# Nearest-neighbour upsampling on one core: the order of the first two loads

## The chip, the cores and the metric

The kernel runs on one core of a Trainium2 chip. The metric is the device time of one execution in microseconds (us). Beside the timed runs there is one profiled execution, whose records give the rows quoted below.

## The reference

The input is 16 images of 64 channels of 64 x 64 float32 values, 16.8 MB. Every value is repeated twice along both axes, so the output is 16 x 64 x 128 x 128, 67.1 MB. There is no arithmetic, only copying:

```python
new_h, new_w = (h * scale_factor, w * scale_factor)
for i in range(new_h):
    for j in range(new_w):
        result[:, :, i, j] = x[:, :, i // scale_factor, j // scale_factor]
```

## The kernel before

Batch, channel and height are flattened to 65,536 image rows of 64 values (256 bytes). Each of the 128 partitions holds R = 512 consecutive rows, 128 KB, and each input row becomes two output rows of 128 values, 1 KB in all. One tile, mem, holds everything in a partition: a free area of 79 expanded rows at the front and the whole input (xt) behind it.

**Loads (L148 to L151).** SyncE issues three loads, one behind the other on its one DMA queue: rows 0 to 8 of each partition (2 KB per partition, 256 KB in all; HEAD is 8), rows 8 to 256 (63,488 bytes per partition, 7,936 KB) and rows 256 to 512 (65,536 bytes per partition). None waits for anything. Each load is split over the 16 DMA engines, eight partitions to an engine.

**Chunks (L160 to L172).** The rows are worked off in nine chunks of 62, 32, 48, 64, 50, 64, 64, 64 and 64 rows. For each chunk VectorE copies the rows into an expanded block u (L170), reading each value and each row twice by a broadcast, and SyncE issues one store of the block (L171). The first chunk is copied in two parts, rows 0 to 31 and 31 to 62; both must be done before its store. The blocks lie in turn at the front of mem and right below the rows that are still unexpanded, over rows already used, so a copy has to wait until the store that last read its place has landed.

**Order.** The framework derives all semaphores from the data: the first copy (rows 0 to 31) waits for the load of rows 0 to 8 and for that of rows 8 to 256; the second copy (rows 31 to 62) needs the latter alone. All nine stores share SyncE's queue with the loads and follow them there.

**Before and after the body.** begin_before_barrier takes the first three instructions of SyncE (EARLY = 3), the three loads, in their order, and puts them ahead of the barrier at the kernel's start. close_early rewrites the end: all semaphores but that of the last store are waited for and cleared by GpSimd, and SyncE alone waits for the last store.

Of the kernel before, what the change touches and what calls it, by code (L numbers as in the profile page):

```python
# [1 line left out]

# [4 lines left out]

EARLY = 3  # L10


def begin_before_barrier(nc):

    blocks = nc.main_func.blocks
    main, body = blocks[0], blocks[1]
    sp = mybir.EngineType.SP
    loads = [i for i in body.instructions if i.engine == sp][:EARLY]  # L20
    for load in loads:
        assert isinstance(load, mybir.InstDMACopy), type(load)
        assert not (load.sync_info and load.sync_info.on_wait)
    names = [i.name for i in loads]
    body.instructions = [i for i in body.instructions if i.name not in names]
    kept = list(main.instructions)
    at = next(
        n
        for n, i in enumerate(kept)
        if i.engine == sp and isinstance(i, mybir.InstDrain)  # L30
    )
    kept[at:at] = loads
    main.instructions = kept


def close_early(nc):

    blocks = nc.main_func.blocks  # L40
    sp, pool = mybir.EngineType.SP, mybir.EngineType.Pool
    stores = [
        i
        for i in blocks[1].instructions
        if i.engine == sp and isinstance(i, mybir.InstDMACopy)
    ]
    last = stores[-1].sync_info.on_update[0].id

    end = list(blocks[-1].instructions)
    wait = end[0]  # L50
    assert wait.engine == sp and isinstance(wait, mybir.InstDrain)
    waits = list(wait.sync_info.on_wait)
    assert len({w.id for w in waits}) == len(waits) > 2
    assert all(w.wait_mode == "sem-ge-imm" for w in waits)

    mine = [i for i in end if i.engine == pool]
    kinds = [type(i).__name__ for i in mine]
    assert kinds == [
        "InstDrain",
        "InstEventSemaphore",  # L60
        "InstEventSemaphore",
        "InstDrain",
        "InstISA",
        "InstDrain",
        "InstEventSemaphore",
        "InstEventSemaphore",
    ], kinds
    d0, gather0, release0, d1, clear, d2, gather1, release1 = mine


    lo, hi = clear.ant_dict["range_first"], clear.ant_dict["range_last"]
    assert lo <= last <= hi and all(lo <= w.id <= hi for w in waits)
    clears = []
    for a, b in ((lo, last), (last + 1, hi + 1)):
        if a < b:
            clears.append(nc.gpsimd.sem_clear(range(a, b)).ins)

    landed = mybir.InstDrain(
        name=wait.name,
        engine=pool,  # L80
        debug=wait.debug,
        sync_info=mybir.SyncInfo(
            on_wait=[w for w in waits if w.id != last], on_update=[]
        ),
    )
    (w,) = [w for w in waits if w.id == last]
    final = mybir.InstEventSemaphore(
        name=clear.name,
        engine=sp,
        debug=wait.debug,  # L90
        sync_info=mybir.SyncInfo(
            on_wait=[w],
            on_update=[
                mybir.SyncUpdate(
                    sync_type=w.sync_type,
                    id=w.id,
                    ant_name=w.ant_name,
                    update_mode="sem-sub-imm",
                    update_value=w.wait_value,
                )  # L100
            ],
        ),
    )
    others = [i for i in end if i.engine != pool and i is not wait]
    blocks[-1].instructions = others + [
        d0, gather0, release0, gather1, release1, d1, landed, *clears, d2, final
    ]


@with_exitstack  # L110
def kernel(
    ctx: ExitStack,
    tc: tile.TileContext,
    x: bass.AP,
    scale_factor: int,
    out: bass.AP,
):
    nc = tc.nc
    nc.at_finalize(begin_before_barrier)
    nc.at_finalize(close_early)  # L120
    P = nc.NUM_PARTITIONS
    s = int(scale_factor)
    B, C, H, W = x.shape
    R = B * C * H // P
    fdt = x.dtype

    xp = x.rearrange("b c h w -> (b c h) w").rearrange("(p r) w -> p r w", p=P)
    op = out.rearrange("b c (h hd) w -> (b c h) (hd w)", hd=s).rearrange(  # L130
        "(p r) w -> p r w", p=P
    )

    rows = [62, 32, 48, 64, 50, 64, 64, 64, 64]
    GROW = s * s
    FREE = 79
    WF = FREE * GROW * W  # L140
    assert sum(rows) == R
    mem_pool = ctx.enter_context(tc.tile_pool(name="mem", bufs=1))
    mem = mem_pool.tile([P, WF + R * W], fdt, name="mem")
    xt = mem[:, WF:].rearrange("p (r w) -> p r w", r=R)

    HEAD = 8  # L148
    cuts = [0, HEAD, R // 2, R]
    for lo, hi in zip(cuts, cuts[1:]):  # L150
        nc.sync.dma_start(out=xt[:, lo:hi], in_=xp[:, lo:hi])  # L151

    def expanded(r0, r1):
        return (
            xt[:, r0:r1].unsqueeze(2).unsqueeze(4).to_broadcast([P, r1 - r0, s, W, s])
        )

    r0 = 0
    before = (0, 0)
    for n, k in enumerate(rows):  # L160
        size = k * GROW * W
        at = 0 if n % 2 == 0 else WF + r0 * W - size
        assert at >= before[1] or at + size <= before[0]
        before = (at, at + size)
        u = mem[:, at : at + size].rearrange(
            "p (k a w b) -> p k a w b", k=k, a=s, w=W
        )
        parts = [0, 31, k] if n == 0 else [0, k]
        for a, b in zip(parts, parts[1:]):
            nc.vector.tensor_copy(out=u[:, a:b], in_=expanded(r0 + a, r0 + b))  # L170
        nc.sync.dma_start(out=op[:, r0 : r0 + k, :], in_=u)  # L171
        r0 += k  # L172


# [1 line left out]
_INS = ['x', 'scale_factor']  # L176
_OUTS = [((16, 64, 128, 128), 'float32')]

_NUMBERS = {'scale_factor': 2}


# [26 lines left out]
```

## Time and profile before

| What | Value |
|---|---|
| Timed runs | 197.21, 197.22, 197.28 us; median 197.22 |
| Profiled execution | span 195.8 us, first to last instruction; no time of its own around the span is recorded |
| Median less span | 1.4 us |
| HBM | 16.78 MB read, 67.11 MB written |
| VectorE | 78.0 us busy in 10 copies |

Only one profiled execution exists, so its terms are set against its span, and the 1.4 us are taken as a constant between span and timed run. Rows of the chain of waits are: start, duration, what. A row of the DMA view with the words "share of 16 engines" sums the durations of all packets that start in the window and divides by the window's length times 16; a packet belongs to the window in which it starts, so that a short window can show over 100%. A large packet is one partition's part of a transfer. The packets under 512 bytes are the 4-byte completion writes, one for each engine and transfer. The column "us to landing" counts from the issue on SyncE to the last completion.

### The profile page before, as it was taken

The numbers are of one execution on the slowest core, as the hardware profiler recorded it, in microseconds if no ns is written. First come the engines' busy times: TensorE is split into PE (matmuls) and PEld (weight loads), VectorE is DVE, ScalarE is ACT, GpSimd is POOL, SyncE is SP. The second block draws the span as 40 slices with busy tenths as digits, with TensorE's granted clock in tenths as the row PEclk, the third lists the DMA queues.
The fourth block names the chain that finished last, engine by engine and source line by source line (L and its number), as shares of the span: only waits on it lengthen the run. The fifth ranks groups of instructions, "written<-read, shape, count | busy, mean of one in ns | idle before, by whom it ended". The sixth has DMA issues, their size and how long they took to land.

```text
span 195.8 us, 76 instructions
## 1 busy us (share of the span) xinstructions
DVE 78.0 (40%) x10; POOL 0.2 (0%) x4
## 2 busy tenths in 40 slices
DVE  0000599980007579085008907900890088000000
POOL 0000000000000000000000000000000000000000
DMA  9999999999999999899987989999999999999994
GB/s 456 415 428 415 428 428 428 428 415 415 415 415 428 428 482 482 375 469 495 469 384 345 502 348 455 442 469 482 469 442 428 428 428 442 428 428 428 428 428 214
DMA packets 1728, 83.89 MB, mean 428 GB/s; under 512 B 192, under 2 KB 192, under 8 KB 320
## 3 DMA queue, kind: packets, MB, share of 16 engines
q1 hardware_dynamic: 1728, 83.89, 99.2%
HBM read 16.78 MB, written 67.11 MB: 428 GB/s over the span
## 4 chain that ended last, share of the span: by engine, by line
DMA 60%; DVE 24%; SPq 0%; issue 0%; DVEq 0%
DMA out_dram<-mem 49%; DVE mem L170 24%; DMA mem<-in_x_dram 11%; SPq L151 0%; DVEq L170 0%
## 5 line engine op out<-in xcount | busy, mean ns | idle before, releaser
L170 DVE COPY mem<-mem 128x16384 f32<-128x16384 f32 (+4 forms) x10 | 78.0, 7812 | 87.8 <-DMA out_dram<-mem 65.8
L189 POOL MEMSET const-uint8-127<- 128x1 uint8 x1 | 0.1, 102 | 0.0
L189 POOL MEMSET const-bfloat16-1.0<- 128x1 bf16 x1 | 0.1, 101 | 0.0
L189 POOL MEMSET const-float32-0.0<- 128x1 f32 x1 | 0.1, 98 | 0.2 <-issue 0.2
L189 POOL MEMSET const-float32-1.0<- 128x1 f32 x1 | 0.1, 98 | 0.0
## 6 DMA issues: line engine op xcount, KB each, us to landing
mem<-in_x_dram SPq DMA_DIRECT2D x1, 7936.0 KB, 21.5
out_dram<-mem SPq DMA_DIRECT2D x1, 7936.0 KB, 21.2
out_dram<-mem SPq DMA_DIRECT2D x1, 6400.0 KB, 27.6
out_dram<-mem SPq DMA_DIRECT2D x1, 6144.0 KB, 17.5
out_dram<-mem SPq DMA_DIRECT2D x1, 4096.0 KB, 26.4
mem<-in_x_dram SPq DMA_DIRECT2D x1, 256.0 KB, 2.7
out_dram<-mem SPq DMA_DIRECT2D x5, 29.8
mem<-in_x_dram SPq DMA_DIRECT2D x1, 40.4
```

Source lines behind the costliest of these rows:

```text
L170: nc.vector.tensor_copy(out=u[:, a:b], in_=expanded(r0 + a, r0 + b))
L189: nc = _bacc.Bacc("TRN2", target_bir_lowering=False, num_devices=1)
```

## The change

The 2 KB per partition of rows 0 to 8 are issued second instead of first. The load of rows 8 to 256 becomes the first of the queue; the load of rows 256 to 512 stays third. Sizes, destinations, copies, stores and waits on data stay as they are.

```diff
     HEAD = 8
-    cuts = [0, HEAD, R // 2, R]
-    for lo, hi in zip(cuts, cuts[1:]):
+    for lo, hi in ((HEAD, R // 2), (0, HEAD), (R // 2, R)):
         nc.sync.dma_start(out=xt[:, lo:hi], in_=xp[:, lo:hi])
```

## The prediction

> **What bounds the kernel now.** I read the page first, then the chain of waits, then the DMA view cut into narrow windows at the start, at the end of the first half's load and at the end of the kernel. The page:
>
> ```profile
> span 195.8 us, 76 instructions
> DVE 78.0 (40%) x10; POOL 0.2 (0%) x4
> DMA  9999999999999999899987989999999999999994
> DMA packets 1728, 83.89 MB, mean 428 GB/s; under 512 B 192, under 2 KB 192, under 8 KB 320
> q1 hardware_dynamic: 1728, 83.89, 99.2%
> ```
>
> VectorE works 40% of the span; the 16 DMA engines work 99.2% of it, on one queue. The stretches say at what rate (columns: stretch, its length, DVE, POOL, clock, DMA share, GB/s):
>
> ```profile
> 22.00:38.00 16.00, 16.00 (x2) 0.00 (x0) 1.00 1.00 434
> 100.00:190.00 90.00, 34.78 (x4) 0.00 (x0) 1.00 1.00 435
> ```
>
> At 434.5 GB/s the 83.89 MB need 83.89/0.4345 = 193.1 us of the 195.8. Only 2.7 us are not full-rate transfer, and the change can win or lose only by what it does to these or by tearing a hole into the stream. The chain that ended last (start, us, what) shows how the front hangs together:
>
> ```profile
> 0.00 0.38 SPq L151
> 0.43 21.46 DMA mem<-in_x_dram
> 21.99 16.76 DVE mem L170 x2
> 38.77 21.19 DMA out_dram<-mem
> ```
>
> The chain names the 7,936 KB load, issued second at 0.43, landed at 21.89. VectorE then makes the first store's data in two copies (16.76), and that store is issued at 38.77. This reads as if the issue at 0.00 delayed the rest by 0.43. The DMA view says otherwise.
>
> **The change part by part.** First the issue. SyncE issues three loads; the rows are the line's own (duration min/median/max, first and last start) and the landing times:
>
> ```profile
> L151 SPq DMA_DIRECT2D mem<-in_x_dram x3: 380/420/432, 0.0 to 0.9; - x3
> mem<-in_x_dram SPq DMA_DIRECT2D x1, 7936.0 KB, 21.5
> mem<-in_x_dram SPq DMA_DIRECT2D x1, 256.0 KB, 2.7
> mem<-in_x_dram SPq DMA_DIRECT2D x1, 40.4
> ```
>
> The windows from 0 to 0.99 us and from 0.99 to 1.25 us of the DMA view (packets that start there; share of 16 engines):
>
> ```profile
> DMA packets 0, 0.00 MB, mean 0 GB/s; under 512 B 0, under 2 KB 0, under 8 KB 0
> ...
> DMA packets 17, 0.03 MB, mean 134 GB/s; under 512 B 0, under 2 KB 0, under 8 KB 17
> q1 hardware_dynamic: 17, 0.03, 129.3%
> ```
>
> No packet starts for 0.99 us, then 17 do within 0.26 us. The second load is issued at 0.43, so by the same delay its packets could run from about 1.4 on; the 256 KB load is still being moved then (below). So that issue lies beside the first load's start-up and transfer, and taking the 7,936 KB load to the front saves none of the 0.43. The 256 KB load, now issued at about 0.4, has some 20 us of cover before its turn on the engines comes. That a transfer with long rows takes longer from issue to first packet is not shown: the issue rows (380 for the first, at most 432 for the others) bound it at 0.05 us. Issue: 0, bounds 0 and +0.05.
>
> Next the transfer of the head itself. Windows 1.65 to 1.9 us (2 KB packets alone) and 5 to 19 us (63,488-byte packets alone):
>
> ```profile
> DMA packets 43, 0.09 MB, mean 352 GB/s; under 512 B 0, under 2 KB 0, under 8 KB 43
> q1 hardware_dynamic: 43, 0.09, 90.7%
> ...
> DMA packets 96, 6.09 MB, mean 435 GB/s; under 512 B 0, under 2 KB 0, under 8 KB 0
> q1 hardware_dynamic: 96, 6.09, 100.4%
> ```
>
> A 2 KB packet takes 0.25 x 16 x 0.907 / 43 = 0.084 us, a large one 14 x 16 x 1.004 / 96 = 2.343 us. Each engine has 8 of each in the first half: 0.68 + 18.74 = 19.4 us in either order. Moving the head moves 0.68 us of work from before the large packets to behind them, and VectorE's first copy (rows 0 to 31) needs both loads before and after the change. The sum of work changes by 0.
>
> What can change is the start-up loss. Windows 0 to 1.9 us and 0 to 3 us:
>
> ```profile
> q1 hardware_dynamic: 97, 0.20, 43.8%
> ...
> DMA packets 160, 1.28 MB, mean 426 GB/s; under 512 B 16, under 2 KB 16, under 8 KB 144
> q1 hardware_dynamic: 160, 1.28, 118.4%
> ```
>
> The 97 packets that start before 1.9 us, all 2 KB, cost 1.9 x 16 x 0.438 = 13.3 engine-us instead of 97 x 0.084 = 8.2: 5.1 too much, 0.32 us for each engine. (The first 17 cost 0.26 x 16 x 1.293 / 17 = 0.316 each.) The 63 that follow until 3 us hold the last 31 small ones, 16 completion writes and each engine's first large one; they cost 3 x 16 x 1.184 - 13.3 = 43.5, less 31 x 0.084 = 2.6, so 40.9/16 = 2.55 for a first large packet against 2.343: 0.21 lost. Together the start now loses 0.53 us per engine, in two steps: a cold first read, and the step from small to large packets.
>
> With the large packets first there is one cold start. It costs at least what one cold packet loses, 0.316 - 0.084 = 0.23, and at most the whole 0.53, if the second step is no step of size but the 16 engines beginning to pull at full rate together. I take the middle, 0.35 to 0.4, so a gain of about 0.15 (bounds 0 and 0.3). That price comes back in part at the new place: the stream now goes from large to 2 KB packets and from these to 65,536-byte ones. The trace of before has no such passage in a running stream. The nearest rows bound each: 0.00 (share 1.00 in 22 to 38 us, large packets throughout) and 0.21 (the small-to-large step at the start). The descriptors of both loads will have been waiting for 20 us, which puts it nearer to the lower end: I take 0.1 for the two together, bounds 0 and 0.42.
>
> Here a page speaks against the change. The Trainium skill, HBM Reference, section Latency, gives 0.2 us for an access on average and 2 us at high load. The head's reads would then move from an idle memory to a busy one, and if one such read were exposed the sum would be about 1.8 us worse. No row here shows such an exposure: the stretches above run at share 1.00 under full load.
>
> Then the laggard. Windows 20.8 to 21.2, 21.5 to 21.6, 194 to 195.1, 195.1 to 195.4 and 195.4 to 195.8 us; "under 512 B" counts the completion writes, one per engine and transfer:
>
> ```profile
> DMA packets 30, 0.98 MB, mean 2458 GB/s; under 512 B 15, under 2 KB 15, under 8 KB 15
> ...
> DMA packets 2, 0.07 MB, mean 655 GB/s; under 512 B 1, under 2 KB 1, under 8 KB 1
> ...
> DMA packets 14, 0.00 MB, mean 0 GB/s; under 512 B 14, under 2 KB 14, under 8 KB 14
> ...
> DMA packets 1, 0.00 MB, mean 0 GB/s; under 512 B 1, under 2 KB 1, under 8 KB 1
> ...
> DMA packets 1, 0.00 MB, mean 0 GB/s; under 512 B 1, under 2 KB 1, under 8 KB 1
> ```
>
> Fifteen engines finish the first half before 21.2 us, one not before 21.5; at the very end again one comes last, after 195.4. An engine that is 0.3 us late in the first load is 0.3 us late 174 us later: every engine carries its own lag to the end, and the latest sets the span. Where it fell behind shows in the window 2.4 to 2.6 us, with one packet, the last engine's first large one:
>
> ```profile
> DMA packets 1, 0.06 MB, mean 317 GB/s; under 512 B 0, under 2 KB 0, under 8 KB 0
> ```
>
> That lag arose in the first 2.6 us, in the stretch that the change rewrites. With 16 cold starts some engine will be last again; I take its lag as unchanged, bounds -0.3 (it is gone) and +0.3 (twice as long).
>
> Last the wait. VectorE's first copy waited for two semaphores before and does so after; behind it on VectorE are all copies, behind these on SyncE all stores. If the first half lands later than its engines finish, store 1 comes later. Its cover, from the windows 38.77 to 40.1 and 40.1 to 40.5 us, in which the third load ends:
>
> ```profile
> DMA packets 0, 0.00 MB, mean 0 GB/s; under 512 B 0, under 2 KB 0, under 8 KB 0
> ...
> DMA packets 28, 0.89 MB, mean 2222 GB/s; under 512 B 14, under 2 KB 14, under 8 KB 14
> ```
>
> Store 1 is issued at 38.77, with 0.99 ready at 39.76; the first engine is free of load 3 no earlier than 40.1. The cover is at least 0.34 us, and it moves along with the first half, since load 3 queues right behind that. Only a landing later than the stream by more than 0.34 would leave the engines idle. The rest of the kernel is the same instructions at the same distances. Cost 0.
>
> Sum: issue 0, work 0, start -0.15, passages +0.1, laggard 0, wait 0 = -0.05 us. Span 195.8 becomes 195.75; the timed runs of before lie 1.4 above the profiled span (median 197.22, 197.21 to 197.28), so 197.17, said as 197.15. All terms at their low ends give -0.3 - 0.3 = -0.6, all at their high ends 0.05 + 0.42 + 0.3 = +0.77.
>
> **The rivals.** (1) Faster: the lag belongs to the 2 KB start. Large first packets leave one cold start and no late step to large packets, and both the 0.21 and the laggard's 0.3 go: -0.5, 196.7. For it: the lag was born before 2.6 us, at just that step. Against: large reads have to start cold too.
>
> (2) Slower: 2 KB packets amid a saturated stream can't hide their reads behind one another. It sits at 20 to 22 us, on every engine, and costs 0.23 for each of the 8 packets that runs at the cold packet's 0.316 instead of 0.084. Two such packets make +0.46, 197.7; all 8 would make +1.9, 199.1. It decides from two packets on, if the start gains nothing. For it: 0.32 us of the present start is lost just so, on small packets. Against: from 1.65 us on they run at 0.084 one behind another, and deeper in the stream their descriptors are long there.
>
> (3) The chain taken at its word: the large load issued 0.43 earlier lands 0.43 earlier and all behind it follows, 196.8. Against: the head's 0.68 us of work is still ahead of the landing and ahead of load 3. The order itself is sure: the code that moves the three loads ahead of the barrier keeps the order of the list.
>
> (4) The head's completion arrives late, the cover of 0.34 is used up and store 1 leaves a hole: 0.4 us of hole wants a landing 0.75 later, 197.6. Against: completions of the 256 KB and of the 7,936 KB load both come from the same queue at each engine's end, and both gate the copy today.
>
> **How the numbers follow.** A measurement of this kernel can tell about 0.2%, 0.39 us: below 196.83 is faster, above 197.61 slower. The forecast, no change that can be told, gets 0.50. Rival 1 gets 0.20 and rival 3 0.05: faster 0.25. Rival 2 gets 0.20 and rival 4 0.05: slower 0.25. The range, 196.6 to 197.9, reaches over rival 1's price and both bounds of the sum on either side (-0.6 and +0.7) and leaves out the far end of rival 2. The forecast's own range is 196.85 to 197.6.
>
> **What would show it.** Right: first packets again about 1.0 us after the first issue; in the window 0 to 3 us 16 large packets and a cost for each of 2.6 to 2.9; the first half's completions within 0.3 us of 20.8 to 21.6, VectorE's first copy at 21.6 to 22.3; share 1.00 from 22 us on. The start is wrong if the completions come before 20.7 (rival 1 or 3); the passages if the 2 KB packets near 21 us take clearly more than 0.084 (rival 2); the wait if packets of store 1 start only after a gap behind load 3 (rival 4). The prediction as a whole is wrong if the last completion write moves by more than 0.4 us.

## The result and the profile after

The changed kernel takes 197.51 us (median of 21 runs, 197.36 to 197.87) where the kernel before takes 197.18 us (21 runs, 196.93 to 197.61). The ratio is 1.0017 with a 95% interval of 1.0010 to 1.0023: 0.33 us slower. That is inside the 0.2% that the prediction called no change, and inside its range, but the sign is not the forecast one (-0.05 us), and the interval excludes zero.

The page of the changed kernel:

```profile
span 196.2 us, 75 instructions
DVE 78.0 (40%) x10; POOL 0.2 (0%) x4
DMA  9999999999999999899998989999999999999994
q1 hardware_dynamic: 1728, 83.89, 99.1%
mem<-in_x_dram SPq DMA_DIRECT2D x1, 7936.0 KB, 21.3
mem<-in_x_dram SPq DMA_DIRECT2D x1, 256.0 KB, 21.5
```

The span is 0.4 us longer with the same bytes and the same 78.0 us of VectorE. There is one instruction less: a separate wait of VectorE has gone. The chain (start, us, what) says which:

```profile
0.00 21.34 DMA mem<-in_x_dram
21.34 0.02 issue
21.36 16.76 DVE mem L169 x2
38.12 0.02 issue
38.14 22.18 DMA out_dram<-mem
```

VectorE starts at 21.36, as soon as the 7,936 KB load has landed at 21.34, and 0.63 us earlier than before (21.99). The 256 KB load lands later, at 0.43 + 21.5 = 21.9. The framework has swapped the first chunk's two copies. Rows 31 to 62, which need the large load alone, are now copied first, and rows 0 to 31, which need the 2 KB load too, second. Both copies take 8.4 us, so their durations don't show the swap. The start does: a copy that runs at 21.36, half a microsecond before the 256 KB load has landed, can't be the one that reads rows 0 to 8. So the order of the first two copies and the first wait did not stay as the section on the change had them. Store 1 is issued at 38.14 instead of 38.77.

An earlier store would seem to do no harm, and yet it lands later: 22.18 us after the issue instead of 21.19, which is at 60.32 instead of 59.96. Of the 0.99 us, 0.63 are only a longer time in the queue; 0.36 are a real delay. A part of it arises ahead of the store on the engines. The window 37.6 to 38.7 us of the DMA view holds each engine's last packet of load 3, 16 in all, in every kernel here but one; first before, then after:

```profile
DMA packets 16, 1.05 MB, mean 953 GB/s; under 512 B 0, under 2 KB 0, under 8 KB 0
q1 hardware_dynamic: 16, 1.05, 220.2%
```

```profile
DMA packets 16, 1.05 MB, mean 953 GB/s; under 512 B 0, under 2 KB 0, under 8 KB 0
q1 hardware_dynamic: 16, 1.05, 230.1%
```

Share times 1.1 us is the mean duration of one packet: 2.422 us before, 2.531 us after. The engines lose 0.11 us on the mean in their last load packet, at a time when store 1 is already queued behind it. The loss is uneven, and the engine that ends last decides. The packet that starts last of the 16 (one packet each, window 38.4 to 38.5 before and 38.5 to 38.6 after) takes 0.1 x 16 x share, 2.42 us before and 2.70 after:

```profile
q1 hardware_dynamic: 1, 0.07, 151.1%
```

```profile
q1 hardware_dynamic: 1, 0.07, 168.7%
```

The start differs as well. The windows 0.99 to 1.25, 1.25 to 1.5, 1.5 to 2.1 and 0 to 3 us of the changed kernel:

```profile
DMA packets 10, 0.63 MB, mean 2442 GB/s; under 512 B 0, under 2 KB 0, under 8 KB 0
...
DMA packets 3, 0.19 MB, mean 762 GB/s; under 512 B 0, under 2 KB 0, under 8 KB 0
...
DMA packets 3, 0.19 MB, mean 317 GB/s; under 512 B 0, under 2 KB 0, under 8 KB 0
...
q1 hardware_dynamic: 16, 1.02, 99.5%
```

Ten engines start their first packet in the first 0.26 us, three by 1.5 us and three after. A first packet takes 3 x 16 x 0.995 / 16 = 2.98 us where a later one takes 2.34: 0.64 lost, and late starts on top, against 0.53 in all before. The window 21.25 to 21.9 us shows the outcome, before and after ("under 512 B" are completions):

```profile
DMA packets 2, 0.07 MB, mean 101 GB/s; under 512 B 1, under 2 KB 1, under 8 KB 1
```

```profile
DMA packets 30, 0.68 MB, mean 1043 GB/s; under 512 B 9, under 2 KB 9, under 8 KB 20
```

Nine engines end the first half after 21.25, before the change one did. So two causes offer themselves: a start that is worse for most engines, and a store that is queued too early. A third comes from the prediction: the passages into and out of the 2 KB packets, which now stand in the middle of the stream.

### The profile page after: what moved, and what is told of

Read it like the earlier page. It is cut to its first block, busy times and chain, and to the rows that moved or that the text cites. A ratio compares the mean times of both kernels' runs of the same rounds, so it can differ in the third digit from the quotient of the medians.

```text
span 196.2 us, 75 instructions
## 1 busy us (share of the span) xinstructions
DVE 78.0 (40%) x10; POOL 0.2 (0%) x4
## 4 chain that ended last, share of the span: by engine, by line
DMA 60%; DVE 24%; issue 0%
DMA out_dram<-mem 50%; DVE mem L169 24%; DMA mem<-in_x_dram 11%
## 6 DMA issues: line engine op xcount, KB each, us to landing
mem<-in_x_dram SPq DMA_DIRECT2D x1, 256.0 KB, 21.5
```

## The experiments

Every ratio is against the kernel before on the same chip, whose medians there were 197.03 to 197.05 us. The ratio is not the quotient of the two medians; the two differ by up to 0.0009, or 0.18 us, so that a difference of 0.1 us by the medians says little. Diffs are against the changed kernel where no other is named. Where a run has another number of loads, EARLY is set to that number, so that all loads stay ahead of the barrier.

**No 2 KB load at all.**

```diff
-    for lo, hi in ((HEAD, R // 2), (0, HEAD), (R // 2, R)):
+    for lo, hi in ((0, R // 2), (R // 2, R)):
```

> Two loads only, rows 0 to 256 and 256 to 512; no 2 KB packets at all. Start theory (a first load of large rows starts the engines late and unevenly, which costs the +0.33 us): as slow as the changed kernel, +0.2 to +0.5 us on before (197.4 to 197.7); first packets of the 16 engines spread over 0.8 to 1.0 us as in the changed kernel, against 0.22 us before. Passage theory (2 KB packets in the middle of the running stream cost it): the passages are gone, so as before or up to 0.2 us faster (196.95 to 197.2). Copy-order theory (VectorE's swapped and earlier copies cost it): the copies stand in the old order and start together after one load, so as before.

> The two large loads without any 2 KB load, once more: a large first load by itself. If the large first load causes what remains of the cost with store 1 late (about +0.2 us): +0.1 to +0.25 us on before, median completion of the first half later than 21.40 although 0.07 us of work is saved. If the 2 KB packets in the middle cause it: -0.1 to +0.05 us.

Measured: 197.15 us, ratio 0.9998 (0.9990 to 1.0007), and again 197.13 us, 1.0005 (0.9996 to 1.0014). First packets come about as unevenly as in the changed kernel: 13 of 16 within the first 0.26 us and one after 1.5 us in the first run, 11 and 4 in the second. Yet the kernel is not measurably slower than before. The theory of the start, which wanted at least 0.2 us, fell here; the two others fit the first run. The second run's +0.09 us lies between the two ranges named for it. By itself a large first load costs some 0.1 us by the medians, or nothing. Store 1 was issued at 38.62 and 38.52 us.

**2 KB first, and 2 KB in the middle as well.**

```diff
-    for lo, hi in ((HEAD, R // 2), (0, HEAD), (R // 2, R)):
+    for lo, hi in ((0, HEAD), (2 * HEAD, R // 2), (HEAD, 2 * HEAD), (R // 2, R)):
```

> Rows 0 to 8 first as before, then 16 to 256, then another 2 KB per partition (rows 8 to 16), then 256 to 512. Start theory: as before, -0.1 to +0.1 us, first packets within 0.25 us. Passage theory: as the changed kernel, +0.2 to +0.5 us. Copy-order theory: the copies are swapped here as in the changed kernel and VectorE starts earlier than the last load of the first half lands, so +0.2 to +0.5 us.

Measured: 197.60 us, 1.0027 (1.0017 to 1.0036). That is 0.57 us by the medians. The start theory misses; the passage and the copy-order theories come nearest, a little under. The copies are swapped here too, and the store is issued at 38.20.

**One copy for the first chunk.**

```diff
-        parts = [0, 31, k] if n == 0 else [0, k]
+        parts = [0, k]
```

> The changed order of loads, but the first chunk is one copy of 62 rows, which waits for both loads. Start and passage theories: still +0.2 to +0.5 us. Copy-order theory: as before, 0 to +0.1 us. VectorE's first copy starts at 21.8 to 22.0 us instead of 21.4.

Measured: 198.36 us, 1.0063 (1.0050 to 1.0076), far more than any theory expected. The groups by shape show why, in the kernel before and in this one:

```profile
L170 DVE COPY mem<-mem 128x7936 f32<-128x7936 f32 x2 | 16.7, 8414 | 22.0 <-DMA mem<-in_x_dram 22.0
```

```profile
L169 DVE COPY mem<-mem 128x15872 f32<-128x15872 f32 x1 | 8.4, 8427 | 21.9 <-DMA mem<-in_x_dram 21.9
```

One copy of 62 rows takes as long as one of 31 rows. The Trainium skill, VectorE: DVE Perf Modes, section Mode 2x_2P, says that a copy runs at two results a cycle only if its outermost dimension longer than 1 is even (or odd and equal in source and destination); the two durations agree with it, 7,936 results in 8.414 us and 15,872 in 8.427. So with parts of 31 rows the first chunk takes 16.8 us, and in one piece 8.4, and store 1 goes out at 30.32, over seven us before the last packets of load 3 start. The window 37.6 to 38.7 us:

```profile
q1 hardware_dynamic: 16, 1.05, 323.8%
```

3.238 x 1.1 = 3.56 us for each last packet of load 3 instead of 2.42. VectorE stands idle meanwhile (stretch, its length, DVE busy first), so its copies can't be what slows them:

```profile
38.00:42.00 4.00, 0.00 (x0) 0.00 (x0) 1.00 1.13 418
```

This gave the theory that the runs behind the next one test: a store that waits in the queue behind a load stretches the load's last packet.

**Only the first load ahead of the barrier (EARLY = 1).**

> The changed order, but only the first load is issued ahead of the barrier; the 2 KB load and the load of the second half follow after it, some 1 us later. If the engines' first packets come late because the descriptors of the next two loads are written at the same time: first packets within 0.3 us of each other and a time of 0 to +0.15 us on before. If they come late because large reads of the first engines hold up the rest, whatever is issued behind: spread still 0.8 to 1.0 us and +0.2 to +0.5 us.

Measured: 197.46 us, 1.0017 (1.0005 to 1.0028). Thirteen engines start in the first 0.26 us, where the changed kernel's first trace had ten; but a second trace of the changed kernel (the run beside the second with a late store, below) has thirteen too, so the number varies from one execution to the next and the edit is not shown to move it. The time stays that of the changed kernel. The store was issued at 37.95; the last packets of load 3 took 2.394 x 1.1 = 2.63 us.

**The kernel before, with store 1 early.** No load is touched; only the first chunk's parts change, so that the copies take 16.3, 15.2 or 8.4 us (behind each line stands when store 1 was issued):

```diff
-        parts = [0, 31, k] if n == 0 else [0, k]
+        parts = [0, 29, 58, k] if n == 0 else [0, k]    # 38.10
+        parts = [0, 25, 50, k] if n == 0 else [0, k]    # 36.96
+        parts = [0, k]                                  # 30.34
```

> The loads of before, head first; the first chunk in parts of 29, 29 and 4 rows, of which the last should be fast (62 rows in one copy took 8.43 us, 31 rows 8.41), so that store 1 is issued at about 38.3 us instead of 38.8. Early-store theory: +0.1 to +0.3 us, with last packets of load 3 that take up to 0.3 us longer. Passage theory: as before, within 0.1 us, since no 2 KB packet has moved.

> As the run with parts of 29, 29 and 4, with parts of 25, 25 and 12 rows: store 1 at about 37.2 us. Early-store theory: between the two others, +0.4 to +1.1 us. Passage theory: as before, within 0.1 us.

> The loads of before; the first chunk in one copy of 62 rows, so that store 1 is issued at about 30.4 us, eight us before load 3 ends. Early-store theory: +1.0 to +1.3 us, as in the run with one copy under the changed order, and every engine's last packet of load 3 stretched by about 1.1 us. Passage theory: as before, within 0.1 us.

Measured: 197.51 us, 1.0026 (1.0011 to 1.0041); 198.17 us, 1.0053 (1.0038 to 1.0068); 198.41 us, 1.0064 (1.0050 to 1.0077). By the medians that is +0.46, +1.12 and +1.36 us, each a little over the early-store theory's range and far from the passage theory's 0.1. The chain of the first, the one with a store at 38.10, and its last packets of load 3 (37.6 to 38.7 us):

```profile
21.79 16.29 DVE mem L170 x3
38.10 21.92 DMA out_dram<-mem
```

```profile
q1 hardware_dynamic: 16, 1.05, 236.9%
```

The other two, in the same window:

```profile
q1 hardware_dynamic: 16, 1.05, 300.4%
```

```profile
q1 hardware_dynamic: 16, 1.05, 327.2%
```

| Store 1 issued at | Mean last packet of load 3 | Kernel | Median |
|---|---|---|---|
| 38.77 | 2.42 us | before | 197.03 to 197.18 |
| 38.52 to 38.62 | 2.43 | no 2 KB load | 197.13, 197.15 |
| 38.56 to 38.81 | 2.42 | changed, store late (below) | 197.36 to 197.41 |
| 38.54 | 2.43 | 2 KB first and in the middle, store late (below) | 197.20 |
| 38.20 | 2.47 | 2 KB first and in the middle | 197.60 |
| 38.05, 38.14 | 2.53 | changed, twice | 197.57, 197.51 |
| 38.10 | 2.61 | before, parts 29, 29, 4 | 197.51 |
| 37.95 | 2.63 | changed, EARLY = 1 | 197.46 |
| 36.96 | 3.30 | before, parts 25, 25, 12 | 198.17 |
| 30.34 | 3.60 | before, one part | 198.41 |
| 30.32 | 3.56 | changed, one part | 198.36 |

With the loads untouched, a store that is issued as early as in the changed kernel (38.10 against 38.14) costs as much as the whole change by the medians. Its 12 runs are spread, though: four lie at 197.16 to 197.22 us, the others at 197.46 or above, and the profile is of a run of 197.22, in which the last packets lost 0.18 us on the mean. The stretch doesn't grow in proportion: a store 1.8 us early costs the last packets 0.88 us, one 8.4 us early 1.18. The mean doesn't give the time by itself: with the store at 38.20 it rises by 0.05 us alone, but the packet that starts last (window 38.6 to 38.7) takes 0.1 x 16 x 1.722 = 2.76 us.

**The changed order with store 1 late.** The chunk is cut at row 7, so that its first copy needs the load that lands last; three times:

```diff
-        parts = [0, 31, k] if n == 0 else [0, k]
+        parts = [0, 7, k] if n == 0 else [0, k]
```

> The changed order of loads, but the first chunk is cut at row 7 instead of 31, so that its first copy already needs the 2 KB load that lands last; both parts stay odd and slow, so store 1 should be issued at 38.7 to 38.8 us as before, not at 38.1. Early-store theory (a store that waits in the queue while the last packets of the load ahead of it still run stretches these; the changed kernel issues store 1 0.6 us earlier): the eighth 65,536-byte packet of load 3 takes 2.42 us again on every engine, and the time is 0 to +0.15 us on before. Passage theory (the 2 KB packets in the middle cost it): still +0.25 to +0.4 us.

> The changed kernel once more, on the chip of the next three: +0.25 to +0.45 us on before; last packets of load 3 stretched by 0.1 us on the mean and up to 0.5 us on single engines, as in its first profile.

> The changed order with the first chunk cut at row 7 (store 1 at 38.6 to 38.8 us), once more, beside the changed kernel. If the early store is the larger part of the change's cost: 0 to +0.15 us on before and at least 0.15 us below the changed kernel. If the large first load and the 2 KB packets in the middle are the larger part: +0.2 to +0.3 us, within 0.1 us of the changed kernel.

> The changed order with store 1 late, beside the two: +0.1 to +0.3 us on before, as twice already. It should be about the sum of the other two if both parts cost independently.

Measured: 197.41 us, 1.0012 (1.0003 to 1.0020); 197.36 us, 1.0009 (0.9993 to 1.0026); 197.39 us, 1.0017 (1.0008 to 1.0025). The changed kernel beside the second of these took 197.57 us, 1.0024 (1.0012 to 1.0037). The late store's time misses its theory: +0.36 us by the medians in the first run (+0.24 by the ratio), where 0 to +0.15 was expected. The second, at +0.31 (+0.18 by the ratio), lies 0.21 below the changed kernel beside it, as that theory wanted, but over its range too, and the third is at +0.35. The changed kernel itself, at +0.52, came out above the range named. The packets do as the theory said. All three issue store 1 at 38.56 to 38.81, and load 3's last packets are whole again, in each of them

```profile
q1 hardware_dynamic: 16, 1.05, 219.8%
```

which is 2.418 us. Of the 34 runs 11 lie below 197.2 us, where none of the 32 runs of the changed kernel lies (197.35 at least); the other 23 lie between 197.24 and 197.9. Late issue brings back some 0.2 of 0.5 us by the medians of the two that ran side by side, not all; the intervals of their ratios overlap. The profile of the third belongs to a run of 197.02 us and has a span of 195.7, that of the second to 197.54 us and 196.2, with a whole last packet in both: the second's store packets are a little longer. The windows 41 to 57 us, second and third (the mean packet is 16 x 16 x share / count: 2.346 and 2.342 us):

```profile
DMA packets 103, 6.54 MB, mean 409 GB/s; under 512 B 0, under 2 KB 0, under 8 KB 0
q1 hardware_dynamic: 103, 6.54, 94.4%
```

```profile
DMA packets 107, 6.79 MB, mean 425 GB/s; under 512 B 0, under 2 KB 0, under 8 KB 0
q1 hardware_dynamic: 107, 6.79, 97.9%
```

Why some executions run like the one and some like the other is not settled.

**The 2 KB packets in the middle, alone.** Four of them behind a shortened large load, and the second experiment's loads with its store late (cut at row 13):

```diff
+    for lo, hi in ((0, 8), (40, R // 2), (32, 40), (8, 16), (16, 24), (24, 32), (R // 2, R)):
```

> Head first as before; the large load of the first half is shortened to rows 40 to 256 and four 2 KB loads follow it, issued so that both copies need the last of them (store 1 stays late). A 2 KB packet takes 0.084 us where 2 KB of a large packet take 2,342/31 = 0.0755 ns x 1,000, so eight more of them in each of four loads cost 8 x 0.0085 = 0.07 us a load: +0.28 us by work alone, median completion of the first half near 21.7 us. If every such load costs a passage of 0.1 us and more besides: +0.6 to +1.0 us, median completion at 22.0 or later. If one passage into small packets costs once, however many follow: +0.35 to +0.5 us.

> Head first, rows 16 to 256, then 2 KB of rows 8 to 16, then the second half; the first chunk cut at row 13, so that both copies need the third load and store 1 is issued at 38.7 to 38.9 us. Only the 2 KB packets in the middle remain of the changed kernel. Without the early store the +0.57 us of the run with the same loads should fall to: 0 to +0.1 us if the large first load is what remains, +0.15 to +0.3 us if the 2 KB packets in the middle are.

Measured: 197.28 us, 1.0003 (0.9990 to 1.0016), and 197.20 us, 1.0007 (0.9993 to 1.0022). Four loads of 2 KB packets in the middle cost 0.23 us by the medians and 0.06 by the ratio, no more than the 0.28 that their work was worked out to; no price for a passage is left. The window 20.6 to 20.9 us of the first:

```profile
DMA packets 67, 0.12 MB, mean 396 GB/s; under 512 B 9, under 2 KB 9, under 8 KB 67
q1 hardware_dynamic: 67, 0.12, 103.2%
```

Less 9 completions of 0.009 us, the 58 small packets take (0.3 x 16 x 1.032 - 0.08)/58 = 0.084 us each, as at the kernel's start. And the loads that cost +0.57 us with the store at 38.20 cost +0.16 us with the store at 38.54 (chain of this run):

```profile
21.77 16.76 DVE mem L169 x2
38.54 21.32 DMA out_dram<-mem
```

That pair, the same loads with an early and a late store, is the nearest to a test of the store alone: 0.40 us by the medians, though on two chips and with intervals that overlap a little (1.0017 to 1.0036 and 0.9993 to 1.0022). The +0.16 left lies in the range expected if the 2 KB packets in the middle remain, but no change at all lies in its interval too.

**An early store behind small packets.** The loads of before with the last 8 rows of the second half as a fourth load, and one copy for the first chunk (against the kernel before):

```diff
-    cuts = [0, HEAD, R // 2, R]
+    cuts = [0, HEAD, R // 2, R - HEAD, R]
-        parts = [0, 31, k] if n == 0 else [0, k]
+        parts = [0, k]
```

> The loads of before, but the last 8 rows of the second half are a fourth load of 2 KB packets; the first chunk in one copy, so that store 1 is queued eight us early. If the early store costs a fixed time where loads end and stores begin: +1.0 to +1.3 us again. If it slows the load packet that runs as the last ahead of it, in proportion to that packet (2.42 us became 3.6): the small last packets lose little, +0.1 to +0.3 us.

Measured: 198.21 us, 1.0056 (1.0036 to 1.0075): +1.16 us by the medians, as expected of a fixed time. The last large packet starts before 37.9 us here (window 37 to 37.9) and takes 0.9 x 3.697 = 3.33 us instead of 2.34; the small ones behind it are slow as well (window 40.5 to 41.6 us: 119 small packets, 23 completions and the first 6 store packets):

```profile
DMA packets 16, 1.02 MB, mean 1129 GB/s; under 512 B 0, under 2 KB 0, under 8 KB 0
q1 hardware_dynamic: 16, 1.02, 369.7%
...
DMA packets 148, 0.62 MB, mean 568 GB/s; under 512 B 23, under 2 KB 23, under 8 KB 142
q1 hardware_dynamic: 148, 0.62, 151.4%
```

Less 6 x 2.342 and 23 x 0.009 us the small ones take (1.1 x 16 x 1.514 - 14.3)/119 = 0.104 us, not 0.084. With eight to an engine the loss is 0.99 + 0.16 = 1.15 us, as with a large last packet. It is not a share of the very last packet: it falls on whatever load is moved in the last four us ahead of the store, and comes to some 1.2 us in all when the store is eight us early. What in the engine does it, the runs don't show.

## Why the prediction was wrong

**The step that failed is the wait**, costed at 0. The prediction said that VectorE's first copy needs both loads before and after the change, and that only a landing later than the stream could cost anything. The copies were swapped, the copy that now runs first waits for the large load alone, and store 1 went out 0.63 us earlier; the first copy's start, 21.36, lies ahead of the 21.6 to 22.3 that the prediction named. The unsaid premise that an earlier store is harmless, because it only queues, was wrong too. Load 3's last packets lost 0.11 us on the mean and 0.28 on the engine that ends last. How much of the change that is, has no single number. An early store alone, under the old order of loads, gave +0.46 us (ratio 1.0026); another pair with the same loads differs by 0.40 us by the medians; the changed order itself gets back only 0.2 when its store is late.

That the time fell inside the stated range owes to the range's width: neither of the two terms that were given a price, the start (-0.15) and the passages (+0.1), came out so, and the term that moved the time stood at 0. (The sum's own high end, +0.77, would be 197.99 us, a little over the range's 197.9.)

**The start** was forecast at -0.15 us, bounds 0 and -0.3. The changed kernel's profile has it the other way: 0.64 us lost per first packet instead of 0.53 in all, and nine late completions instead of one. Large packets first start the engines less evenly, not more. By itself it does little: without any 2 KB load the time was +0.12 and +0.09 us by the medians, and both intervals include no change.

**The passages** were forecast at +0.1 us for two. The 2 KB packets run at 0.084 us in the middle of the stream. In the changed kernel, 20.6 to 20.75 us:

```profile
DMA packets 26, 0.04 MB, mean 287 GB/s; under 512 B 5, under 2 KB 5, under 8 KB 26
q1 hardware_dynamic: 26, 0.04, 75.4%
```

Less five completions that is (0.15 x 16 x 0.754 - 0.045)/21 = 0.084. Rival 2 falls, and the 2 us that the Trainium skill, HBM Reference, section Latency, gives for an access at high load are not exposed there.

**The laggard** was taken as unchanged. Engines do carry their lag to the end, as said, but a new lag can arise at load 3's end. In the changed kernel's trace the last engine ends the first half at 21.64 (before 21.52) and loses another 0.28 us in its last packet of load 3: 0.40 us together, which is what the last completion moved by (195.84 against 195.44). These are one execution of each kernel. Four completions come after 195.4 us instead of one (windows 194 to 195.4 and 195.4 to 196.2):

```profile
DMA packets 12, 0.00 MB, mean 0 GB/s; under 512 B 12, under 2 KB 12, under 8 KB 12
...
DMA packets 4, 0.00 MB, mean 0 GB/s; under 512 B 4, under 2 KB 4, under 8 KB 4
```

**Right were** the issue and the work. The first packets again start about 1.0 us after the first issue. The large load did land 0.55 us earlier (21.34 against 21.89), as rival 3's reading wants, and nothing was won by it. Rival 4 had the right place, the end of load 3, and the wrong direction: store 1 was not late, it was early.

**Open** is the rest, 0.3 us by the medians that the changed order keeps with store 1 late. Its two halves measured +0.09 and +0.12 (large load first) and +0.16 us (2 KB in the middle); they could add up to it, but every interval of theirs includes no change. With the 0.40 to 0.46 us of an early store alone the parts come to more than the whole change, 0.33 and 0.52 us in its two measurements, so the shares are not settled. No kernel of the study beats the one before.

## What to carry to other kernels

Reordering loads changes which operations become ready first, and the framework may swap work behind it, as it did here: compare the order and waits of the two programs before costing anything at nothing. In a kernel that is bound by the DMA queue, an operation that finishes earlier need not be harmless: look at what it then puts into the queue, and beside what. The Trainium skill, DMA: Bandwidth & Descriptors, section Rules for kernel authors, advises, to overlap a DMA with compute, to issue it early and to wait for it late; here a store issued 0.67 us earlier behind a running load cost 0.46 us by the medians.

## What was not expected of the hardware

A store queued behind a load slows the load's end: 2.42 us became 3.60 for the last 65,536-byte packet of every engine when the store was eight us early, 2.61 when it was 0.67 us early. A VectorE copy of 31 rows takes as long as one of 62 (8.414 and 8.427 us), so the two odd parts of the first chunk are what holds store 1 back until the load is nearly done.
